# Whole chunks instead of halves in the cached-page attention of a two-layer decoder step

## Chip, cores and metric

The kernel runs on one core of a Trainium2 chip. The metric is the device time of one execution in microseconds (us), here the median over the runs. Below, PE is TensorE's matmuls, PEld its weight loads, DVE is VectorE, ACT is ScalarE, POOL is GpSimd, SP is SyncE, which issues most DMAs.

## The reference, cut to what matters

One inference step of a decoder trunk of two layers, for 256 prompt tokens and 8 samples of 8 new tokens each. A layer is half a SwiGLU network, a mixer, and half a SwiGLU network again. The mixer has three groups of heads (HGRN2, RWKV-7 and MLA attention). The change lies in MLA attention of the samples, which reads a paged cache of 16 pages of 128 tokens for every sample:

```python
def mla_sample_attn(q_nope, q_pe, c, k_pe, ckv_pages, kpe_pages, wuk, wuv):
    c_past = ckv_pages.reshape(B, -1, MLA_KV_RANK)
    kpe_past = kpe_pages.reshape(B, -1, MLA_ROPE)
    q_lat = jnp.einsum('bqhd,rhd->bqhr', q_nope, wuk)
    s_past = jnp.einsum('bqhr,bkr->bhqk', q_lat, c_past) + jnp.einsum('bqhe,bke->bhqk', q_pe, kpe_past)
    ...
    pr = jax.nn.softmax(s, axis=-1)
    o_lat = jnp.einsum('bhqk,bkr->bqhr', pr[..., :P], c_past) + ...
    return jnp.einsum('bqhr,rhd->bqhd', o_lat, wuv)
```

## The kernel before

All matrices are fp32. Activations are kept transposed, 320 tokens wide. A dense product (`dense_steps`, line 398) takes a 128x128 weight block and issues three matmuls of 320 columns on a high and a low part that ScalarE and VectorE split off (`split`, line 422).

**The mixer (line 550) is a weave of streams.** Each stream is a Python generator that emits some instructions and then yields the time at which it may go on, in the kernel's own planning time `self.pe`. `mm` (line 283) adds a planned cost for each matmul: 0.2475 for one of 256 columns onto 64 output rows. `weave` (line 513) takes the first stream of its list whose time has come; where none has, it moves planning time ahead to the earliest. So the order of the instructions in the program is written by due times. A first weave holds `rw` (urgent), `sample`, `fill` (the dense input products of RWKV and HGRN) and `rws`; a second holds `hg` (urgent), `sample`, `prompt` (urgent) and `w_out`. The framework's scheduler then lays that order out for each engine: it takes the program's order as the priority, puts instructions of urgent streams ahead, and takes later instructions where earlier ones are not ready by its own reckoning.

**The sample stream (line 821)** handles the 8 samples in 4 pairs `p`; a pair's cache is 4 chunks `ch` of 4 pages for each of its two samples `si`.

- `scores(p, ch)` (line 851) loads the transposed latents `ct` in tiles of 2 pages of one sample (two DMAs each) and multiplies them with `qlat`: 12 matmuls of 96x256 onto 64 output rows, alternating between the two samples, whose results lie in the two halves of the partitions. Every fp32 matmul is shown as two instructions, so a chunk shows 24.
- `values(p, ch)` (line 892) loads the plain latents `cn`, again in tiles of 2 pages, transposes the exponentials `S` into `PT`, and adds 8 matmuls (16 instructions) onto the accumulator `po` in the bank `pv`.
- `ct` and `cn` have 5 buffers each. A chunk needs 4 tiles of its kind. The order of the stream is four chunks of scores of pair 0, then values of pair p and scores of pair p+1 in turn, then four chunks of values of pair 3 alone. After each pair follow a softmax remainder and the division (lines 944 to 961); at the end the stream loads `wuv` into two `cn` buffers (line 966) and multiplies the result out.

Before the change both kinds go by **halves**: two tiles, then the matmuls that read them. `ready` (line 836) gives a half its due time: 4 pages at 1.05 after the due time of the half before it, or after the planned end of the half three before it, whichever is later; then 2.2 for landing. All page loads are issued by SP. `pages` (line 842) reads the page numbers into SP registers. The last part of the output product that needs the samples (`w_out`, line 590) waits for the end of the stream, the event `smp`.

Of the kernel before, what the change touches and what calls it, by code (L numbers as in the profile page):

```python
# [26 lines left out]
RANK = 256  # L27
# [5 lines left out]
PAGE = 128  # L33
NPAGE = 16
# [2 lines left out]

FBLK, MBLK = 8, 4
LEVELS = [32, 16, 8, 4, 2, 1]
PACE = (0, 1.05)  # L40
ORDER_A = lambda fill, sample: (sample, fill)
ORDER_B = lambda prompt, sample: (sample, prompt)

# [213 lines left out]
class Kern:  # L257
# [563 lines left out]
    def sample(self):  # L821
        nc, l = self.nc, self.l
# [11 lines left out]
        feed = {"ct": [20.0, [], 0], "cn": [20.0, [], 0]}  # L834

        def ready(name, n):
            f = feed[name]
            f[0] = max(f[0], f[1][f[2] - 3] if f[2] > 2 else 0.0) + n * (PACE[1] if f[2] < PACE[0] else 1.05)
            f[2] += 1
            return 0, f[0] + 2.2  # L840

        def pages(i, n):

            with self.tc.issue_after(self.gat[-8].ins) if len(self.gat) >= 8 else ExitStack():
                return nc.values_load_multi_w_load_instructions(
                    self.pti[0:1, i:i + n], engines=[mybir.EngineType.SP], min_val=0, max_val=NPOOL - 1,
                    skip_runtime_bounds_check_because="a page table names pages of the pool")[1]
# [2 lines left out]

        def scores(p, ch):
            ps = self.bank("pa")
            for hf in range(2):
                yield ready("ct", 4)
                self.mark(f"sample{l}")
                cts = []
                for si in range(2):
                    ct = self.s([KR, 2, 3 * PAGE], "ct", 5)
                    i0 = (2 * p + si) * NPAGE + ch * 4 + hf * 2
                    for pg, r in enumerate(pages(i0, 2)):  # L860
                        self.gat.append(nc.sync.dma_start(ct[:, pg, :], ctp[bass.ds(r + l * NPOOL, 1)].rearrange("a p c -> p (a c)")))
                    cts.append(ct)
                for kt in range(3):
                    for si in range(2):
                        self.mm(ps[64 * si:64 * si + 64, hf * 256:hf * 256 + 256], qlat[:KR, kt, 2 * p + si],
                                cts[si][:, :, kt * PAGE:kt * PAGE + PAGE], start=kt == 0, stop=kt == 2)
                feed["ct"][1].append(self.pe)
            S[p, ch] = self.s([128, 512], "S", 5)
            if ch == 0:
                mx[p] = self.s([128, 8], "smx", 2)  # L870
            nc.scalar.copy(S[p, ch], ps)
            nc.vector.tensor_reduce(out=mx[p][:, ch:ch + 1], in_=S[p, ch], axis=AX.X, op=ALU.max)
# [15 lines left out]
        def exps(p, ch):  # L888
            m = mx[p]
            nc.scalar.activation(S[p, ch], S[p, ch], AF.Exp, bias=m[:, 5:6], scale=MLA_SCALE, accum_out=m[:, ch:ch + 1])  # L890

        def values(p, ch, po):
            r0 = ready("cn", 4)
            cns_ = []
            rs = []
            for si in range(2):
                i = (2 * p + si) * NPAGE + ch * 4
                rs.append(pages(i, 4))
            for hf in range(2):
                for si in range(2):  # L900
                    cn = self.s([128, 2, RANK], "cn", 5)
                    for pg in range(2):
                        r = rs[si][hf * 2 + pg]
                        self.gat.append(nc.sync.dma_start(cn[:, pg, :], self.ap["cn"][l, bass.ds(r, 1)].rearrange("a p c -> p (a c)")))
                    cns_.append(cn)
            yield 0, r0[1] - 1.5
            self.mark(f"sample{l}")
            if ch < 3:
                exps(p, ch + 1)
            pt = self.bank("pa")  # L910
            for pg in range(4):
                self.tr(pt[:, pg * 128:pg * 128 + 128], S[p, ch][:, pg * 128:pg * 128 + 128], idt)
            PT = self.s([128, 512], "PT", 2)
            nc.vector.tensor_copy(PT, pt)  # L914
            yield 0, max(self.pe + 1.2, r0[1])
            for hf in range(2):
                self.mark(f"sample{l}")
                for pg in (2 * hf, 2 * hf + 1):
                    for si in range(2):
                        self.mm(po[64 * si:64 * si + 64, :RANK], PT[:, pg * 128 + 64 * si:pg * 128 + 64 * si + 64],  # L920
                                cns_[2 * hf + si][:, pg % 2, :], start=ch == 0 and pg == 0, stop=False)
                feed["cn"][1].append(self.pe)
                if hf == 0:
                    yield ready("cn", 4)

        for ch in range(4):
            yield from scores(0, ch)
# [3 lines left out]
        for p in range(4):  # L931
            po = self.bank("pv")
            exps(p, 0)
            for ch in range(4):
                yield from values(p, ch, po)
                if p < 3:
                    yield from scores(p + 1, ch)
# [31 lines left out]
        for g in range(4):  # L969
            ps = self.bank("pa")  # L970
            for rt in range(2):
                for hh in range(2):
                    h = 2 * g + hh
                    self.mm(ps[64 * hh:64 * hh + 64, :64], wuv[rt][:, h * 64:h * 64 + 64], qlat[:, rt, :, h, :],
                            start=rt == 0, stop=rt == 1)
# [546 lines left out]
```

## Time and profile before

| | us |
|---|---|
| median of 3 runs | 1676.75 (1676.6 to 1680.71) |
| the profiled execution | 1678.2 |
| its span, first to last instruction | 1676.4 |
| PE busy | 1627.8 (97%) |
| PEld busy | 1448.2 (86%) |
| DVE busy | 958.7 (57%) |
| ACT busy | 716.8 (43%) |

The profile is of one execution on the one core. Busy time of PE is the time in which at least one matmul was in flight; matmuls are pipelined, so a busy PE can still be slower than its best. "Idle before" is the time for which an engine had nothing in flight before an instruction, with what released it. In the timeline view one row merges neighbouring instructions of one group: start, length, engine, line, operation, output and inputs, shapes, count. A start-to-start distance between two rows is the time that the first of them really took from the engine.

### The profile page before, as it was taken

The numbers are of one execution on the slowest core, as the hardware profiler recorded it, in microseconds if no ns is written. First come the engines' busy times: TensorE is split into PE (matmuls) and PEld (weight loads), VectorE is DVE, ScalarE is ACT, GpSimd is POOL, SyncE is SP. The second block draws the span as 40 slices with busy tenths as digits, with TensorE's granted clock in tenths as the row PEclk, the third lists the DMA queues.
The fourth block names the chain that finished last, engine by engine and source line by source line (L and its number), as shares of the span: only waits on it lengthen the run. The fifth ranks groups of instructions, "written<-read, shape, count | busy, mean of one in ns | idle before, by whom it ended". The sixth has DMA issues, their size and how long they took to land. (4 is left out here: it accounts for less than half of the span.)

```text
span 1676.4 us, 33385 instructions
## 1 busy us (share of the span) xinstructions
PE 1627.8 (97%) x13174; PEld 1448.2 (86%) x13174; DVE 958.7 (57%) x1599; ACT 716.8 (43%) x1209; POOL 78.3 (5%) x112
## 2 busy tenths in 40 slices
PE   8999999999999899999999999999999998999998
PEld 7999998777557599999999999987765666999998
DVE  7555447844456575554465554478344665655543
ACT  6444334543353354443344443346242543544433
POOL 0000000200031000000000000002000300000000
PEclk9999999999999999999999999999999998999999
DMA  8555526556573454555445555456457545345542
GB/s 268 151 151 149 149 81 175 173 150 178 177 229 112 150 171 149 151 151 151 151 145 149 149 151 150 115 161 185 118 172 217 160 135 180 112 147 147 150 151 93
DMA packets 130908, 260.05 MB, mean 155 GB/s; under 512 B 17264, under 2 KB 75952, under 8 KB 130624
## 3 DMA queue, kind: packets, MB, share of 16 engines
q1 hardware_dynamic: 111584, 223.58, 44.7%
q10 hardware_dynamic: 19136, 34.28, 6.9%
q8 instruction: 104, 1.70, 0.4%
q0 software_dynamic: 32, 0.07, 0.1%
q14 instruction: 52, 0.43, 0.1%
HBM read 253.39 MB, written 4.47 MB: 154 GB/s over the span
## 5 line engine op out<-in xcount | busy, mean ns | idle before, releaser
L423 DVE TENSOR_TENSOR w<-raw,w 128x1024 fp32r<-128x1024 f32 (+1 forms) x392 | 410.0, 1047 | 325.9 <-ACT w L422 319.8
L422 ACT CAST w<-raw 128x1024 fp32r<-128x1024 f32 (+1 forms) x392 | 354.9, 909 | 437.4 <-PE pd L286 190.3
L286 PE MATMUL pd<-xh,w 128*128 128x320 f32 x1792 | 427.6, 317 | 14.4 <-ACT w L422 10.6
L286 PEld LDWEIGHTS pd<-xh,w 128*128 128x128 f32 x1792 | 307.0, 190 | 30.6 <-ACT w L422 14.9
L286 PE MATMUL pd<-xl,w 128*128 128x320 f32 x896 | 282.0, 316 | 0.0
L286 PE MATMUL pr<-xh,w 128*128 128x320 f32 x1056 | 241.7, 311 | 4.4 <-ACT w L422 4.0
L286 PE MATMUL pa<-xh,w 128*128 128x320 f32 x896 | 201.7, 309 | 0.0
L286 PEld LDWEIGHTS pr<-xh,w 128*128 128x128 f32 x1056 | 178.3, 188 | 6.6 <-ACT w L422 5.3
L286 PEld LDWEIGHTS pd<-xl,w 128*128 128x128 f32 x896 | 170.5, 190 | 5.6 <-issue 4.6
L286 PE MATMUL pr<-xl,w 128*128 128x320 f32 x528 | 162.5, 309 | 0.0
L286 PE MATMUL pd<-hh,w 128*128 128x320 f32 x704 | 158.2, 309 | 0.0
L286 PE MATMUL pr<-hh,w 128*128 128x320 f32 x704 | 158.2, 309 | 0.0
L286 PEld LDWEIGHTS pa<-xh,w 128*128 128x128 f32 x896 | 151.0, 188 | 0.0
L286 PE MATMUL pa<-xl,w 128*128 128x320 f32 x448 | 137.6, 309 | 0.0
L286 PE MATMUL pa<-ct,qlat 96*64 96x256 f32 x768 | 119.9, 393 | 0.8 <-ACT w L422 0.4
L286 PEld LDWEIGHTS pd<-hh,w 128*128 128x128 f32 x704 | 118.4, 188 | 0.0
L286 PEld LDWEIGHTS pr<-hh,w 128*128 128x128 f32 x704 | 118.4, 188 | 0.0
L286 PE MATMUL pd<-hl,w 128*128 128x320 f32 x352 | 108.8, 309 | 0.0
L286 PE MATMUL pr<-hl,w 128*128 128x320 f32 x352 | 108.8, 309 | 0.0
L286 PEld LDWEIGHTS pr<-xl,w 128*128 128x128 f32 x528 | 99.1, 188 | 0.4
L470 ACT ACTIVATE fa<-fa 128x320 f32<-128x320 f32 x88 | 41.5, 472 | 134.0 <-DVE fa L469 133.9
L286 PEld LDWEIGHTS pa<-ct,qlat 96*64 96x64 f32 x768 | 59.9, 138 | 38.3 <-issue 14.2
(381 smaller groups left out, 2010.4 us busy)
## 6 DMA issues: line engine op xcount, KB each, us to landing
raw<-in_wf SPq DMA_DIRECT2D x264, 512.0 KB, 3.6
ct<-in_ct SPq DMA_DIRECT2D x256, 144.0 KB, 2.8
raw<-in_wm ACTq DMA_DIRECT2D x128, 256.0 KB, 3.1
cn<-in_cn SPq DMA_DIRECT2D x256, 128.0 KB, 2.4
xT<-in_x SPq DMA_DIRECT2D x4, 320.0 KB, 6.9
wukt<-in_wukt SPq DMA_DIRECT2D x2, 576.0 KB, 6.3
S<-in_rws SPq DMA_DIRECT2D x4, 256.0 KB, 3.5
o_rws<-S SPq DMA_DIRECT2D x4, 256.0 KB, 2.7
```

The source lines that it names most:

```text
L286: self.last = self.nc.tensor.matmul(out, w, x, start=start, stop=stop)
L422: self.cast = nc.scalar.copy(h, src).ins
L423: nc.vector.tensor_tensor(out=lo, in0=src, in1=h.bitcast(F32), op=ALU.subtract)
L470: nc.scalar.activation(a, a, AF.Silu)
```

## The change

`scores` and `values` take a whole chunk at a time: four tiles are loaded, then all matmuls of the chunk follow in one piece, in the reverse order (second half first, second sample first), so that the first matmul reads the tile that was issued last. `ready` gives a chunk its due time as 8 pages at 1.05 after its predecessor's due time or after the planned end of its predecessor's matmuls, whichever is later, plus 2.2. The stream yields once less in each chunk. For the last pair, chunks 1 and 3 of the values take buffers of `ct`. The numbers of loads, matmuls and transposes stay as they are.

```diff
-PACE = (0, 1.05)
+PACE = 1.05
...
         def ready(name, n):
             f = feed[name]
-            f[0] = max(f[0], f[1][f[2] - 3] if f[2] > 2 else 0.0) + n * (PACE[1] if f[2] < PACE[0] else 1.05)
+            f[0] = max(f[0], f[1][f[2] - 1] if f[2] else 0.0) + n * PACE
             f[2] += 1
             return 0, f[0] + 2.2
...
         def scores(p, ch):
             ps = self.bank("pa")
+            yield ready("ct", 8)
+            self.mark(f"sample{l}")
+            cts = []
             for hf in range(2):
-                yield ready("ct", 4)
-                self.mark(f"sample{l}")
-                cts = []
                 for si in range(2):
                     ct = self.s([KR, 2, 3 * PAGE], "ct", 5)
-                    i0 = (2 * p + si) * NPAGE + ch * 4 + hf * 2
-                    for pg, r in enumerate(pages(i0, 2)):
+                    rs = pages((2 * p + si) * NPAGE + ch * 4 + hf * 2, 2)
+                    for pg, r in enumerate(rs):
                         self.gat.append(nc.sync.dma_start(ct[:, pg, :], ctp[bass.ds(r + l * NPOOL, 1)].rearrange("a p c -> p (a c)")))
                     cts.append(ct)
+
+            for hf in (1, 0):
                 for kt in range(3):
-                    for si in range(2):
+                    for si in (1, 0):
                         self.mm(ps[64 * si:64 * si + 64, hf * 256:hf * 256 + 256], qlat[:KR, kt, 2 * p + si],
-                                cts[si][:, :, kt * PAGE:kt * PAGE + PAGE], start=kt == 0, stop=kt == 2)
-                feed["ct"][1].append(self.pe)
+                                cts[2 * hf + si][:, :, kt * PAGE:kt * PAGE + PAGE], start=kt == 0, stop=kt == 2)
+            feed["ct"][1].append(self.pe)
...
         def values(p, ch, po):
-            r0 = ready("cn", 4)
+            r0 = ready("cn", 8)
...
-                    cn = self.s([128, 2, RANK], "cn", 5)
+
+                    cn = self.s([128, 2, RANK], "ct" if p == 3 and ch % 2 else "cn", 5)
...
             yield 0, max(self.pe + 1.2, r0[1])
-            for hf in range(2):
-                self.mark(f"sample{l}")
-                for pg in (2 * hf, 2 * hf + 1):
-                    for si in range(2):
-                        self.mm(po[64 * si:64 * si + 64, :RANK], PT[:, pg * 128 + 64 * si:pg * 128 + 64 * si + 64],
-                                cns_[2 * hf + si][:, pg % 2, :], start=ch == 0 and pg == 0, stop=False)
-                feed["cn"][1].append(self.pe)
-                if hf == 0:
-                    yield ready("cn", 4)
+            self.mark(f"sample{l}")
+            for pg in (3, 2, 1, 0):
+                for si in (1, 0):
+                    self.mm(po[64 * si:64 * si + 64, :RANK], PT[:, pg * 128 + 64 * si:pg * 128 + 64 * si + 64],
+                            cns_[2 * (pg // 2) + si][:, pg % 2, :], start=ch == 0 and pg == 3, stop=False)
+            feed["cn"][1].append(self.pe)
```

## Rows read from the trace of the kernel before

**Rows 1.** Windows by stage: us, busy time of each engine, granted clock, DMA.
```profile
0.00:250.00 250.00, 242.40 (x1631) 241.31 (x1632) 142.00 (x215) 109.84 (x152) 3.10 (x9) 1.00 0.53 159
250.00:592.00 342.00, 327.46 (x3295) 239.06 (x3293) 200.87 (x401) 145.47 (x316) 36.10 (x50) 0.99 0.57 170
592.00:1080.00 488.00, 487.36 (x3315) 486.26 (x3315) 275.81 (x388) 211.25 (x284) 0.00 (x0) 1.00 0.48 144
1080.00:1418.00 338.00, 321.89 (x3248) 233.90 (x3247) 197.73 (x395) 141.15 (x309) 36.12 (x50) 0.97 0.57 167
```

**Rows 2.** What PE waited for: us in total, times, longest.
```profile
PE pa L290 <- ACT S L890: 6.4, 4, 1.9
PE pv L286 <- DMA cn<-in_cn: 4.3, 4, 2.6
PE pa L286 <- DMA ct<-in_ct: 0.4, 1, 0.4
```

**Rows 3.** Timeline of PE, first layer: first sample run, then one whole chunk.
```profile
294.91 1.95 PE L286 MATMUL pa<-ct,qlat 96*64 96x256 f32 x16
...
329.37 0.31 PE L286 MATMUL pd<-xh,w 128*128 128x320 f32 x1
329.61 2.81 PE L286 MATMUL pa<-ct,qlat 96*64 96x256 f32 x24
332.36 0.42 PE L286 MATMUL pd<-xh,w 128*128 128x320 f32 x1
332.61 0.31 PE L286 MATMUL pd<-xl,w 128*128 128x320 f32 x1
332.75 0.45 PE L286 MATMUL pd<-xh,w 128*128 128x320 f32 x2
```

**Rows 4.** Timeline of PE, first layer: one chunk of values, cut up.
```profile
371.08 0.31 PE L286 MATMUL pd<-xh,w 128*128 128x320 f32 x1
371.32 0.65 PE L286 MATMUL pv<-cn,PT 128*64 128x256 f32 x2
371.89 0.68 PE L286 MATMUL pr<-X,rwa 64*64 64x64 f32 x16
372.50 0.65 PE L286 MATMUL pv<-cn,PT 128*64 128x256 f32 x4
373.09 0.68 PE L286 MATMUL pr<-rwa,X 64*64 64x64 f32 x16
```

**Rows 5.** Timeline of PE, first layer: end of the sample stream.
```profile
552.90 1.95 PE L286 MATMUL pv<-cn,PT 128*64 128x256 f32 x16
554.78 0.66 PE L290 MATMUL pa<-cf,S 128*128 128x128 f32 x4
...
567.30 1.32 PE L286 MATMUL pv<-cn,PT 128*64 128x256 f32 x6 [0.62 <-DMA cn<-in_cn]
...
570.57 0.82 PE L286 MATMUL pd<-pPT,V 128*64 128x256 f32 x8
571.95 0.65 PE L286 MATMUL pv<-cn,PT 128*64 128x256 f32 x2 [0.56 <-DMA cn<-in_cn]
```

**Rows 6.** Timeline of PE, second layer: first and last run of sample matmuls.
```profile
1121.09 1.95 PE L286 MATMUL pa<-ct,qlat 96*64 96x256 f32 x16
...
1399.81 0.65 PE L286 MATMUL pv<-cn,PT 128*64 128x256 f32 x2 [2.55 <-DMA cn<-in_cn]
```

**Rows 7.** Timeline of SP, first layer: page loads in mid-stream and at its end.
```profile
452.22 4.90 SPq L904 DMA_DIRECT2D cn<-in_cn  x8
...
540.62 27.13 SPq L904 DMA_DIRECT2D cn<-in_cn  x31
567.85 0.85 SPq L966 DMA_DIRECT2D cn<-in_wuv  x2
568.88 0.34 SPq L904 DMA_DIRECT2D cn<-in_cn  x1
```

**Rows 8.** View of the tile cn: from issue to landing.
```profile
DMA to landing us min/median/max: 1.9/2.4/6.9
```

**Rows 9.** Windows at the ends of both layers' streams: columns as in the first group.
```profile
575.10:578.50 3.40, 3.40 (x22) 2.57 (x16) 0.45 (x2) 0.42 (x2) 0.00 (x0) 0.51 0.00 0
1396.00:1401.00 5.00, 2.45 (x19) 1.11 (x18) 0.85 (x2) 0.37 (x1) 0.00 (x0) 1.00 0.29 93
1401.10:1411.30 10.20, 9.22 (x53) 7.37 (x54) 2.85 (x8) 1.84 (x6) 0.00 (x0) 0.50 0.16 31
```

More of the change, by code (lines that the diff above doesn't have):

```diff
@@ L892, in values @@
         def values(p, ch, po):
-            r0 = ready("cn", 4)
+            r0 = ready("cn", 8)
             cns_ = []
-            rs = []
-            for si in range(2):
-                i = (2 * p + si) * NPAGE + ch * 4
-                rs.append(pages(i, 4))
+            rs = [pages((2 * p + si) * NPAGE + ch * 4, 4) for si in range(2)]
             for hf in range(2):
                 for si in range(2):
-                    cn = self.s([128, 2, RANK], "cn", 5)
+                    cn = self.s([128, 2, RANK], "ct" if p == 3 and ch % 2 else "cn", 5)
                     for pg in range(2):
@@ L915, in values @@
             yield 0, max(self.pe + 1.2, r0[1])
-            for hf in range(2):
-                self.mark(f"sample{l}")
-                for pg in (2 * hf, 2 * hf + 1):
-                    for si in range(2):
-                        self.mm(po[64 * si:64 * si + 64, :RANK], PT[:, pg * 128 + 64 * si:pg * 128 + 64 * si + 64],
-                                cns_[2 * hf + si][:, pg % 2, :], start=ch == 0 and pg == 0, stop=False)
-                feed["cn"][1].append(self.pe)
-                if hf == 0:
-                    yield ready("cn", 4)
+            self.mark(f"sample{l}")
[4 more added lines that the diff above has]
+            feed["cn"][1].append(self.pe)
         for ch in range(4):
```

## The prediction

> **What bounds the kernel now.** I read the windows by stage first, to see where PE loses time at all. The two networks around the mixer leave PE next to nothing to gain: 487.36 of 488.00 us busy. The mixers take 342 and 338 us, with 327.46 and 321.89 busy, so PE stands still for 14.5 and 16.1 us in them [rows 1]. The DMA engines are at 0.57 of their time there, so bandwidth is no bound. PE is the engine to watch, and a change can bring time in two ways: less standing still, or a PE that gets through the same matmuls faster while it counts as busy.
>
> The list of waits comes second. Of the idle time, waits for pages are a small part: 4.3 us for `cn` and 0.4 for `ct` in both layers together; the waits for the exponentials (6.4 us) aren't touched by the change [rows 2]. So what was to be gained from pages that land earlier is under 5 us.
>
> Third, the timeline of PE. A chunk of scores that runs in one piece takes from 329.61 to 332.36, 2.75 us for its 24 instructions or 0.115 each [rows 3]. Such chunks are rare. A chunk of values at 371 us is cut after 2 instructions, then after 4, with matmuls of the RWKV stream between [rows 4]. Taking any unbroken stretch of `ct` or `cn` matmuls as a run, I count 76 runs in the first layer, the first and last being those at 294.91 and 571.95 us [rows 3, 5], and 76 in the second, from 1121.09 to 1399.81 [rows 6]. Whole chunks would need 32 a layer.
>
> Last, the end of the stream, where nothing else is left for PE. In the first layer SP issues the last 32 page loads from 540.62 to 569.22, with only the two `wuv` loads in between [rows 7]; that is 28.6 us or 7.2 for each chunk of 8 loads. In mid-stream 8 loads take SP 4.90 us [rows 7]. So at the end the five `cn` buffers hold the loads back, and PE waits 0.62 and 0.56 us there, in the second layer 2.55 [rows 5, 6].
>
> **The change, part by part.** The sum is made against the profiled execution, 1678.2 us with a span of 1676.4. It lies 1.45 above the median, which I take off at the end. No load, matmul, transpose or copy is added or removed.
>
> *Fewer cuts.* What a cut costs: 2 instructions hold PE from 371.32 to 371.89, 0.57 us where 2 x 0.115 = 0.23 would do, so 0.34 too much; 4 hold it 0.59 where 0.46 would do, 0.13 too much [rows 4]. The mean is 0.24. Going in costs as well: from a dense matmul to a sample matmul it is 0.24 us from start to start, between two dense ones 0.14 to 0.15 [rows 3, 4], so 0.09 more. A cut costs 0.33. Two things cut: a tile that the scheduler doesn't hold for landed when the one before it is (the first matmul then runs alone), and urgent matmuls of other streams. Waiting for the last tile first takes away the first kind only. I take 44 runs a layer, 32 chunks and a dozen urgent cuts: 2 x 32 x 0.33 = 21.1 us less. Bounds: all 44 cuts a layer gone, 29.0; only 12 a layer, 7.9.
>
> *The waits for pages* (4.7 us, [rows 2]) go, since most stood at the stream's end, where the loads will be arranged otherwise; what comes in their place is the next point.
>
> *Later due times.* This works against the change. A half was due 4.2 after the half before, so 8.4 for a chunk. Now a chunk is due 8.4 + 2.2 after the end of the last chunk of its kind and takes 12 x 0.2475 = 2.97 (scores) or 1.98 (values). Sixteen chunks of scores and four of values alone come to at least 16 x 13.57 + 4 x 12.58 = 267 of the planner's own microseconds where 20 x 8.4 = 168 was the pace asked for. The planner fills that time with the other streams, which are then used up earlier, and the sample's chunks slide towards the end. On the chip the stream takes 277 us in the first layer even now (294.91 to 572), so urgent work delays it anyway, and I don't carry over the whole difference. I take it that of the last four chunks of values three have nothing beside them. With two sets of buffers in turn, such a chunk costs SP's 4.90 us for its 8 loads, and PE has 1.88 (552.90 to 554.78) and some 0.66 of transposes to do [rows 5]; 2.4 us stay empty. That is 7.2 a layer, 14.4 in all. Bounds: nothing, if the stream keeps its place, and without turns 4.90 + 2.4 for landing [rows 8] less 2.5 = 4.8 a chunk for all four, 38 us in all.
>
> *The keys' buffers for the last values* let the loads of chunk 1 start as soon as the last scores are done and not after chunk 0 of the values: 4.90 for a chunk in place of 7.2 [rows 7]. This is in the term above already; without it the 2.4 would be 4.6.
>
> *One wait for a chunk.* Scores of a chunk now wait for its 8th load, half of them waited for the 4th: up to half of SP's 4.90 us later. In mid-stream PE has other streams for that time, so I set nothing; without cover it would be 2.45 us a chunk. Queued behind the waiting matmul are the copy of `S` and its maximum, which are needed a whole pair later. On SP the loads of the other kind are queued behind a load that waits for a buffer; three of a chunk's four tiles wait for the chunk before, so both kinds come in bursts of 8. That has the same cover.
>
> *The clock.* Before the second layer's end PE was busy for 2.45 of 5.00 us, and after it the granted clock was 0.50 for 10.2 us, which is 1.2 GHz; in the first layer it was 0.51 for 3.4 us [rows 9]. A thinner end in the first layer may bring one more stretch of 3.4 us at half clock: 1.7 us.
>
> Sum: -21.1 - 4.7 + 14.4 + 1.7 = -9.7. From 1678.2 that is 1668.5, and less 1.45, **1667**.
>
> **The rivals.** *The late stream (slower).* The dense fill is used up early, and the last two pairs of chunks as well as all four chunks of values run bare. A bare pair costs SP 2 x 4.90 = 9.8 us and PE 2.75 + 1.88 + 0.66 = 5.3, so 4.5 idle; with 4 x 2.4 that is 18.6 a layer, 37.2 in all: +37.2 - 21.1 - 4.7 + 1.7 = +13, or 1690. It decides from 12.9 idle us a layer on, where it eats up both gains. For it speaks the sum of due times; against it that the stream is already longer than those due times, and that the scheduler takes ready chunks ahead when PE is free.
>
> *Nothing moves (same).* The cuts are mostly urgent work, as in [rows 4], and stay; 12 fewer a layer give 7.9, and two bare chunks a layer cost 9.6: 9.6 - 7.9 - 4.7 + 1.7 = -1.3, or 1675. For it: both cuts in [rows 4] are followed by RWKV matmuls, which are urgent.
>
> *The low clock (slower).* The bare chunks at the end are short bursts between loads; if PE goes through them and through the part of the output product behind them at 0.50, as after 1401 us, that product (8 tiles of 6 matmuls at 0.15, 7 us) takes twice as long in both layers, while the chunks stay hidden behind their loads: 14 us in place of 1.7, so +2.6 against the profiled time, or 1678 to 1679; with one more bare chunk a layer it is 1684. The Trainium skill ("TensorE: Matmul & The Clock Gate", section on HAM oscillation) says that bursts of matmuls with DMA waits between them start at the low clock every time. The trace agrees for the one stretch it shows, at 1401 us. By that rule the sum would be this rival's and not mine.
>
> **How the numbers follow.** What a measurement of this kernel can tell from no change is 0.3%, 5 us. My forecast gets 0.43; its own range is 1648 to 1672. Nothing moves: 0.18. The late stream: 0.35, the low clock: 0.04; both slower. The two main terms have the same size and opposite signs, so the range has to hold both: from 1647 (all cuts gone, no chunk bare: 1678 - 29 - 4.7 and a little back) to 1700 (the late stream with half of the cuts left). Beyond lies 0.2.
>
> **What the profile after would show.** If the cuts go: chunks of 24 and 16 instructions in one piece, under 50 runs a layer, and fewer busy microseconds of the `ct` and `cn` groups. If the late stream holds: page loads that end later relative to `prompt` and `w_out`, with PE idle and waiting for `cn` in the last 30 us of each mixer. If nothing moves: about 70 runs a layer, with RWKV matmuls between. I am wrong if the mixers shorten by other means than these, or if PE waits for pages in mid-stream, where I set nothing.

## The result and the profile after

The changed kernel takes 1759.57 us (median of 4 runs, 1755.61 to 1766.97) against 1676.67 us in the same comparison: a ratio of 1.0501, interval 1.0481 to 1.0522. It is slower by 83 us. The forecast was 1667, and even the upper end of the range, 1700, lies 60 us below the result. The profiled execution took 1755.61.

The page of the changed kernel, span and engines:

```profile
span 1753.8 us, 33367 instructions
...
PE 1647.9 (94%) x13174; PEld 1476.6 (84%) x13174; DVE 954.0 (54%) x1599; ACT 712.8 (41%) x1203; POOL 78.6 (4%) x112
```

Against before the span grew by 77.4 us. PE stands still for 1753.8 - 1647.9 = 105.9 us where it stood for 48.6, so 57.3 us of the loss is idle time and 20.1 is time in which PE counts as busy. Next, the windows by stage, with the columns of [rows 1]; the mixers now end at about 632 and 1495 us:

```profile
250.00:632.00 382.00, 335.13 (x3267) 250.69 (x3266) 196.27 (x396) 140.96 (x309) 36.16 (x50) 0.91 0.51 150
632.00:1124.00 492.00, 492.00 (x3351) 491.34 (x3350) 279.42 (x394) 213.58 (x287) 0.00 (x0) 1.00 0.49 145
1124.00:1495.00 371.00, 327.17 (x3230) 242.25 (x3229) 193.20 (x393) 138.57 (x305) 36.30 (x50) 0.93 0.51 152
```

The mixers took 342 and 338 us [rows 1]; now they take 382 and 371, and their granted clock fell from 0.99 and 0.97 to 0.91 and 0.93. The network between them is nearly as it was (492 us here, 488 before). What PE waited for (us in total, times, longest), the rows that answer to [rows 2]:

```profile
PE pa L286 <- DMA ct<-in_ct: 42.8, 15, 5.9
PE pv L286 <- DMA cn<-in_cn: 10.7, 6, 4.2
...
PE pv L286 <- DMA ct<-in_cn: 7.8, 2, 3.9
```

Waits for pages were 4.7 us and are 61.3. That is +56.6, about as much as the idle time gained. So the place is found: pages that come too late for PE, in both layers alike (33.2 and 28.1 us). Why they are late is read from two views that group PE's work by what it is. First the stretch from 250 to 400 us, early in the first layer's stream, in the kernel before:

```profile
L286 PE MATMUL pd<-xh,w 128*128 128x320 f32 x185 | 46.6, 324 | 1.4 <-ACT w L422 0.6 <-DVE pe L1002 0.5 <-DVE w L423 0.2
...
L286 PE MATMUL pa<-ct,qlat 96*64 96x256 f32 x168 | 25.6, 390 | 0.0
...
L286 PE MATMUL pv<-cn,PT 128*64 128x256 f32 x48 | 9.1, 395 | 0.0
```

And the same stretch in the changed kernel:

```profile
L286 PE MATMUL pd<-xh,w 128*128 128x320 f32 x260 | 62.1, 318 | 1.1 <-DVE w L423 0.7 <-ACT w L422 0.4
...
L286 PE MATMUL pa<-ct,qlat 96*64 96x256 f32 x120 | 18.4, 393 | 0.0
...
L286 PE MATMUL pv<-cn,PT 128*64 128x256 f32 x16 | 1.9, 379 | 0.0
```

No page is waited for here. PE does other things: 75 more of the dense matmuls `pd<-xh,w`, and of the sample's work two chunks of scores and two of values less (48 and 32 instructions). That work comes back later, when little dense work is left beside it. It begins in mid-stream: from 400 to 470 us, with 24 `pd<-xh,w` where the kernel before has 65, PE waits 11.1 us for pages, in the second layer 10.1 us from 1270 to 1320. Most of it comes at the end, when nothing dense is left. The same grouping from 520 to 620 us, changed kernel:

```profile
L286 PE MATMUL pa<-ct,qlat 96*64 96x256 f32 x144 | 26.6, 525 | 13.8 <-DMA ct<-in_ct 13.8
L286 PE MATMUL pv<-cn,PT 128*64 128x256 f32 x128 | 21.4, 481 | 7.6 <-DMA cn<-in_cn 4.4 <-DVE PT L914 3.1
...
L286 PE MATMUL pv<-ct,PT 128*64 128x256 f32 x32 | 4.5, 426 | 3.9 <-DMA ct<-in_cn 3.9
...
L286 PE MATMUL pd<-xh,w 128*128 128x320 f32 x2 | 0.9, 552 | 0.0
```

Six chunks of scores and ten of values run in these 100 us, and two dense matmuls `pd<-xh,w`. What a pair of chunks costs when it is alone is seen in PE's timeline of that stretch:

```profile
564.42 4.23 PE L286 MATMUL pa<-ct,qlat 96*64 96x256 f32 x24 [3.54 <-DMA ct<-in_ct]
568.58 0.95 PE L290 MATMUL pa<-cf,S 128*128 128x128 f32 x4
570.32 1.95 PE L286 MATMUL pv<-cn,PT 128*64 128x256 f32 x16 [0.78 <-DVE PT L914]
575.76 4.59 PE L286 MATMUL pa<-ct,qlat 96*64 96x256 f32 x24 [3.49 <-DMA ct<-in_ct]
...
588.20 5.32 PE L286 MATMUL pa<-ct,qlat 96*64 96x256 f32 x24 [4.54 <-DMA ct<-in_ct]
```

And in SP's, which issues the loads:

```profile
556.67 5.63 SPq L861 DMA_DIRECT2D ct<-in_ct  x8
562.85 4.54 SPq L904 DMA_DIRECT2D cn<-in_cn  x8
568.09 5.66 SPq L861 DMA_DIRECT2D ct<-in_ct  x8
574.29 5.56 SPq L904 DMA_DIRECT2D cn<-in_cn  x8
580.56 5.63 SPq L861 DMA_DIRECT2D ct<-in_ct  x8
```

A pair takes PE 11.3 and 12.4 us from start to start. SP takes 11.4 and 12.5 us for the 16 loads of a pair, and the rows of loads fill all but some 1.3 us of it. SP hardly waits for buffers here; from 556 to 591 us its list of waits has one row:

```profile
SPq L861 <- PE pv L286: 0.7, 3, 0.3
```

So SP's issue is the bound, and PE waits. The 16 DMA instructions are only part of it, 0.32 to 0.35 us each in most cases, some 5.5 us a pair; reading the page numbers into registers takes 0.47 us six times, 2.8 us. PE is also slow while it works: 24 instructions take 4.23 to 5.32 us where [rows 3] showed 2.81. The windows (columns as in [rows 1]) give the reason:

```profile
520.00:560.00 40.00, 30.26 (x179) 17.58 (x180) 12.58 (x26) 9.78 (x22) 1.32 (x1) 0.70 0.52 150
560.00:600.00 40.00, 25.16 (x155) 18.67 (x151) 6.12 (x15) 5.29 (x14) 0.00 (x0) 0.79 0.65 189
```

The granted clock is 0.70 and 0.79, a mixture of the levels 1.2 and 2.4 GHz, while PE is busy for 30 and 25 us of 40. Within a pair the scores, after a wait of 3.5 us, get the low clock for part of their time, and the values behind them the full one:

```profile
564.40:568.60 4.20, 4.18 (x25) 3.37 (x25) 0.00 (x0) 0.00 (x0) 0.00 (x0) 0.67 0.84 223
570.30:572.30 2.00, 1.95 (x16) 1.05 (x16) 0.56 (x1) 0.00 (x0) 0.00 (x0) 1.00 0.53 155
```

### The profile page after: what moved, and what is told of

It reads as the page before. It is cut to its first block, busy times and chain, and to the rows that moved or that the text cites. A ratio compares the mean times of both kernels' runs of the same rounds, so it can differ in the third digit from the quotient of the medians.

```text
span 1753.8 us, 33367 instructions
## 1 busy us (share of the span) xinstructions
PE 1647.9 (94%) x13174; PEld 1476.6 (84%) x13174; DVE 954.0 (54%) x1599; ACT 712.8 (41%) x1203; POOL 78.6 (4%) x112
## 4 chain that ended last, share of the span: by engine, by line
PE 84%; DMA 5%; SPq 5%; issue 2%; DVE 2%; ACT 2%; DVEq 0%; ACTq 0%
PE pd L286 32%; PE pr L286 29%; PE pa L286 19%; PE pv L286 3%; DMA ct<-in_ct 2%; SPq L861 2%; DMA raw<-in_wm 2%; SPq L845 1%; PE pa L290 1%; SPq L904 1%; PE pd L290 0%; DMA xT<-in_x 0%; DVE w L423 0%; DMA ct<-in_cn 0%; DMA raw<-in_wf 0%
## 5 line engine op out<-in xcount | busy, mean ns | idle before, releaser
L286 PE MATMUL pd<-xh,w 128*128 128x320 f32 x1792 | 420.3, 315 | 13.8 <-ACT w L422 10.0
L286 PE MATMUL pa<-ct,qlat 96*64 96x256 f32 x768 | 129.4, 457 | 42.8 <-DMA ct<-in_ct 42.8
L286 PEld LDWEIGHTS pa<-ct,qlat 96*64 96x64 f32 x768 | 78.8, 161 | 76.0 <-issue 52.1
```

The lines of the kernel that those rows point to most:

```text
L286: self.last = self.nc.tensor.matmul(out, w, x, start=start, stop=stop)
```

## The experiments

Ratios are to the kernel before, run in turn with each on the same chip (medians of 1675.0 to 1677.5 us), with their 95% intervals.

### Undo the due rule in the changed kernel; put the rule alone into the kernel before

**Two back.**

```diff
-            f[0] = max(f[0], f[1][f[2] - 1] if f[2] else 0.0) + n * PACE
+            f[0] = max(f[0], f[1][f[2] - 2] if f[2] > 1 else 0.0) + n * PACE
```

> The changed kernel with one index of the due-time rule put back in spirit: a chunk is due after the planned end of the chunk two before it, not of the one just before (the rule before the change looked three halves back). Whole chunks, the reverse order and the extra buffers stay. Theory A (the due times push the chunks of the sample behind all other work): the last 90 us of a mixer with nothing but sample work on PE shrink to 10 or 20, the time goes back to 1660 to 1695 us. Theory B (whole chunks themselves are the cost: four of five buffers bound to a chunk, so loads and matmuls of a kind can't overlap): the stream stays slow, 1735 to 1760. With A, the time against the kernel before the change also tells what whole chunks are worth by themselves.

Measured: 1690.70 us, 1.0079 [1.0054, 1.0105], in the range of theory A. PE's waits for pages:

```profile
PE pa L286 <- DMA ct<-in_ct: 18.7, 13, 3.1
...
PE pv L286 <- DMA cn<-in_cn: 5.8, 2, 3.3
PE pv L286 <- DMA ct<-in_cn: 5.4, 3, 3.4
```

**Halves, late** (on the kernel before; halves, order and buffers stay):

```diff
-            f[0] = max(f[0], f[1][f[2] - 3] if f[2] > 2 else 0.0) + n * (PACE[1] if f[2] < PACE[0] else 1.05)
+            f[0] = max(f[0], f[1][-1] if f[1] else 0.0) + n * 1.05
...
-                yield ready("ct", 4)
+                yield (0, 0.0) if hf else ready("ct", 8)
...
-            r0 = ready("cn", 4)
+            r0 = ready("cn", 8)
...
-                    yield ready("cn", 4)
+                    yield 0, 0.0
```

> The kernel before the change, still by halves in the old order with the old buffers, but with the new due times: the first half of a chunk is due 8.4 + 2.2 after the planned end of the last half of its kind, the second half at once. Theory A: as slow as the changed kernel, 1740 to 1780 us, with a long stretch of bare sample work at the end of each mixer. Theory B: the time stays within 1% of the kernel before the change, 1665 to 1695, since the halves still overlap.

Measured: 1744.28 us, 1.0397 [1.0369, 1.0426]; 23.8 us of waits for `ct`, 14.1 for `cn`, and 260 dense matmuls `pd<-xh,w` from 250 to 400 us, as many as in the changed kernel. The rule alone costs 69 us on the old kernel, and taking it out of the new one gives back 69. This is the main cause, shown from both sides.

### The order alone undone

```diff
-            for hf in (1, 0):
+            for hf in (0, 1):
...
-                    for si in (1, 0):
+                    for si in (0, 1):
...
-            for pg in (3, 2, 1, 0):
-                for si in (1, 0):
+            for pg in (0, 1, 2, 3):
+                for si in (0, 1):
...
-                            cns_[2 * (pg // 2) + si][:, pg % 2, :], start=ch == 0 and pg == 3, stop=False)
+                            cns_[2 * (pg // 2) + si][:, pg % 2, :], start=ch == 0 and pg == 0, stop=False)
```

> The changed kernel with the matmuls of a chunk in the old order (first half first, first sample first), so that the first matmul waits for the tile that lands first. Theory A: 1755 to 1770 us, no gain from the order, since at the end of the mixer SP's issue of 16 loads a pair sets the pace whichever tile comes first. Theory B: the early matmuls overlap with the later loads again, a pair shortens by up to 2 us, 1730 to 1750. If the reverse order keeps chunks in one piece, as I had forecast, this kernel has more runs than the 55 a layer of the changed one, worth 0.33 us each.

Measured: 1758.34 us, 1.0499 [1.0471, 1.0526]: no difference from the changed kernel, as theory A expected. While the stream is late, the order within a chunk doesn't change the time. PE waits less for pages (39.7 us in place of 61.3) and is busy longer (1671.4 us in place of 1647.9), which fits SP's issue setting the pace either way. The sample matmuls fall into 60 runs in each layer, where the changed kernel shows 55 and 54; by the price of 0.33 these are 4 us, too few to see here.

### The keys' buffers

**Taken out of the changed kernel:**

```diff
-                    cn = self.s([128, 2, RANK], "ct" if p == 3 and ch % 2 else "cn", 5)
+                    cn = self.s([128, 2, RANK], "cn", 5)
```

> The changed kernel without the keys' buffers for the last values: all values take the five cn buffers. Both theories: slower by the loads that can't go ahead in the last four chunks of each mixer, 3 chunks of some 4 us, 10 to 25 us in all: 1770 to 1785. Nothing (1755 to 1765) would say that this part of the change was free.

Measured: 1784.19 us, 1.0638 [1.0615, 1.0662], 25 us above the changed kernel. PE's timeline of the last three chunks of values, first layer:

```profile
599.48 3.26 PE L286 MATMUL pv<-cn,PT 128*64 128x256 f32 x16 [2.65 <-DMA cn<-in_cn]
606.62 3.68 PE L286 MATMUL pv<-cn,PT 128*64 128x256 f32 x16 [3.66 <-DMA cn<-in_cn]
613.58 3.68 PE L286 MATMUL pv<-cn,PT 128*64 128x256 f32 x16 [3.27 <-DMA cn<-in_cn]
```

A chunk takes 7 us here and PE waits before each. I read that as loads and matmuls taking turns on one set of buffers.

**Put alone into the kernel before** (the same line, the other way round):

> The kernel before the change with only the keys' buffers for the last values. Theory A (the keys' buffers pay by letting the last loads run ahead, 25 us in the late stream): the last loads of a mixer end some 5 us earlier; the waits for cn (4.3 us) go, 1666 to 1674 us. Rival (the end of the mixer is set by the prompt's heads as well, so earlier values wait for nothing): 1673 to 1679, no difference.

Measured: 1662.00 us (6 runs, 1661.58 to 1663.67), 0.9925 [0.9903, 0.9946]. This beats both kernels, and is better than either expectation. SP's timeline at the end of the first layer's stream:

```profile
539.34 5.78 SPq L904 DMA_DIRECT2D cn<-in_cn  x8
545.65 4.38 SPq L904 DMA_DIRECT2D ct<-in_cn  x8
550.56 5.03 SPq L904 DMA_DIRECT2D cn<-in_cn  x7
...
557.48 3.99 SPq L904 DMA_DIRECT2D ct<-in_cn  x7
561.57 0.38 SPq L966 DMA_DIRECT2D cn<-in_wuv  x1
562.13 0.72 SPq L904 DMA_DIRECT2D ct<-in_cn  x1
```

The last 32 loads go out from 539.34 to 562.85, 23.5 us, where [rows 7] showed 28.6. PE no longer waits for `cn` at all; 2.1 us of waits for `ct` are left. What went is mainly one stop of SP in each layer. SP's waits for PE's values at the end of the first layer's stream, before (540 to 570 us) and here (539 to 563 us):

```profile
SPq L904 <- PE pv L286: 6.5, 2, 6.3
SPq L904 <- PE pv L286: 1.5, 2, 1.1
```

In the second layer the longest stop goes from 8.1 to 2.6 us.

### The reverse order, in the kernel before

**Inside each half, scores and values:**

```diff
-                    for si in range(2):
+                    for si in (1, 0):
...
-                for pg in (2 * hf, 2 * hf + 1):
-                    for si in range(2):
+                for pg in (2 * hf + 1, 2 * hf):
+                    for si in (1, 0):
...
-                                cns_[2 * hf + si][:, pg % 2, :], start=ch == 0 and pg == 0, stop=False)
+                                cns_[2 * hf + si][:, pg % 2, :], start=ch == 0 and pg == 1, stop=False)
```

> The kernel before the change with only the order reversed inside each half: the half's second tile first. Theory of the cuts (0.33 us each, those by landing go away): about 60 runs a layer in place of 76, 8 to 12 us less, 1664 to 1669. Rival (the cuts don't cost PE time that is short, or they are urgent work): 70 or more runs, or fewer runs at 1673 to 1680.

Measured: 1706.35 us, 1.0193 [1.0167, 1.0219]: 31 us slower, outside both ranges. The runs did become fewer as the theory of the cuts had it, 58 and 66 a layer in place of 76 and 76, but the time went the other way: what the order costs is more than the cuts can give. SP and PE at the end of the first layer's stream, first SP:

```profile
546.94 30.05 SPq L904 DMA_DIRECT2D cn<-in_cn  x31
...
579.80 0.34 SPq L904 DMA_DIRECT2D cn<-in_cn  x1
```

then PE:

```profile
571.80 1.08 PE L286 MATMUL pv<-cn,PT 128*64 128x256 f32 x8 [1.06 <-DMA cn<-in_cn]
573.68 1.88 PE L286 MATMUL pv<-cn,PT 128*64 128x256 f32 x8 [0.80 <-DMA cn<-in_cn]
577.29 1.97 PE L286 MATMUL pv<-cn,PT 128*64 128x256 f32 x8 [1.73 <-DMA cn<-in_cn]
582.24 1.97 PE L286 MATMUL pv<-cn,PT 128*64 128x256 f32 x8 [2.97 <-DMA cn<-in_cn]
```

The last 32 loads take 33.2 us in place of 28.6 [rows 7]; the longest stop among them, in which SP waits for PE's values, is 9.6 us in place of 6.3. And the first of them goes out 6.3 us later than before, so the stream was late ahead of its end already. The two tiles of a half are now read as one block that starts with the second one's landing, and the tile that was loaded first is read last, so that its buffer, the one that the next loads ask for first, comes free late. In the old order PE reads a tile while the next one is landing. That is how I read these rows; no run parts the late start from the late release. PE's waits grow towards the end, and from 573.7 on eight instructions take 1.9 us in place of 1.1: from 572 to 584 us the granted clock was 0.58.

**In the values alone** (the `pg` and last `si` lines of that diff):

> The kernel before with the reverse order inside each half in the values alone; the scores keep the old order. Theory (the reverse order costs where loads wait for buffers, which is the values' end: there a buffer pair comes free late, and of the 23.8 us of waits for cn that the reverse order in both kinds showed, 4.3 were there before): 1692 to 1704, with 18 to 24 us of waits for cn. Rival (the scores' reverse order costs it, or both share it in mid-stream): 1676 to 1686, with under 10 us for cn.

Measured: 1696.12 us, 1.0126 [1.0097, 1.0156], with 19.0 us of waits for `cn` and 8.3 for `ct`. As expected by the theory: some 21 of the 31 us lie in the values, and most of the waits for `cn` come in the last chunks of a layer, after 565 and 1406 us.

### Order and buffers together, and whole chunks in the old order

**Reverse order in the halves with the keys' buffers** (both edits above):

> Both of the last two together, halves and old due times kept: if each gives what its theory says, 1655 to 1665 us, which would beat both kernels; by the rivals 1673 to 1680.

Measured: 1691.61 us, 1.0102 [1.0076, 1.0129], slower than either expectation. The buffers give back 15 of the 31 us, no more.

**Whole chunks, old order, two-back rule, keys' buffers** (the edits of the first and the third experiment in the changed kernel):

> The kernel of e1 (whole chunks, due after the planned end of the chunk two before) with the matmuls in the old order, first tile first. If waiting for the last tile first is what costs the remaining 13 us of e1, since PE stands in a chunk that could begin, this one gets 5 to 15 us faster, 1676 to 1686. If one piece is worth more than an early start, it gets slower, 1693 to 1705, with more runs a layer.

Measured: 1673.55 us (12 runs), 0.9992 [0.9979, 1.0006]: no difference from before. Against the two-back run the old order is worth 17 us, in the direction of the first theory and a little beyond its 5 to 15. Against the halves with the keys' buffers (1662.00) whole chunks and their rule lose 11.5 us. Its sample matmuls fall into 74 and 72 runs in the two layers, hardly fewer than 76 and 76; the two-back run, which differs only in the order, shows 56 and 54. So it is the reverse order that joins the cuts here, and not the chunk. (In the late stream the runs are few in the old order too: 60 and 60 above, and 62 and 64 in halves.)

Put in a row, these runs add up to the change: the kernel before, 1675; with the keys' buffers, 1662; with whole chunks and the two-back rule besides, 1674; with the reverse order, 1691; with the change's own rule, 1760. The steps are -13, +12, +17 and +69 us. No run parts whole chunks from the two-back rule within the 12, and the steps hold in this sequence only: in the late stream the order is worth nothing and the buffers 25.

### What in the rule makes the stream late

**Half the pace**, the changed kernel with

```diff
-PACE = 1.05
+PACE = 0.5
```

> The changed kernel with its rule (8 pages after the end of the chunk before), but 0.5 a page in place of 1.05. A chunk of scores is then planned at 2.2 + 8 x 0.5 + 2.97 = 9.2 in place of 13.6. Theory (the planned period is what makes the stream late): 9.2 is under what SP needs for the 16 loads of a pair, so the stream keeps its place; 1690 to 1710, near the 1690.7 of the two-back rule, with the waits for ct back under 25 us. Rival (it is the chaining to the end of the matmuls, whatever the pace): 1740 to 1760.

Measured: 1748.89 us, 1.0451 [1.0417, 1.0485]. The theory I had then, that the period only has to lie under what SP needs for a pair, fell.

**No pace** (`PACE = 0.0`):

> The changed kernel with its rule (after the end of the chunk before), but nothing a page in place of 1.05: a chunk is due 2.2 after the end of its predecessor, planned at 5.2 for scores in place of 13.6, far under what SP needs. Half the pace (9.2) had still shown 1748.9. Theory (the period is what counts, and 9.2 was still too long, since urgent work between comes on top): the stream keeps its place, the last chunk of scores starts before 560 us in the first layer, and the time is near that of the two-back rule, 1680 to 1700. Rival (it is the tie to the predecessor's end, in which every delay stays, whatever the pace): the last chunk of scores starts after 570 us, 1725 to 1750.

Measured: 1693.94 us, 1.0119 [1.0078, 1.0161]; the last chunk of scores of the first layer starts at 551 us. So the tie to the predecessor by itself isn't it either.

**A quarter of it** (`PACE = 0.25`):

> The changed kernel with its rule and 0.25 a page: a chunk of scores is planned at 2.2 + 8 x 0.25 + 2.97 = 7.2, between the 9.2 that showed 1748.9 and the 5.2 that showed 1693.9, and below the 8.4 of the two-back rule (1690.7). Theory (the tie is harmless once the planned period is under 8.4): 1685 to 1705. Rival (the tie carries every delay along, so that the loss shrinks evenly with the pace, and 7.2 lies half way): 1715 to 1735.

Measured: 1728.55 us, 1.0324 [1.0281, 1.0367]: the rival's value, the loss shrinks step by step with the pace. With a planned 7.2 a chunk, less than the 8.4 of the two-back rule, this kernel is still 38 us slower than that one, so the length of the planned period alone doesn't decide.

**The tie with a running clock:**

```diff
-            f[0] = max(f[0], f[1][f[2] - 1] if f[2] else 0.0) + n * PACE
+            f[0] = max(f[0] + n * PACE, f[1][f[2] - 1] if f[2] else 0.0)
```

> The changed kernel, due at the later of 8.4 after its predecessor's due time and the predecessor's planned end, plus 2.2: the tie to the predecessor stays, but the 8.4 run from due time to due time and not from the end of the matmuls. Theory (what made the stream late is that the 8.4 were added behind the end of the matmuls): near the two-back rule, 1685 to 1705. Rival (the tie itself): over 1715.

Measured: 1700.84 us, 1.0134 [1.0099, 1.0170]: the theory's value. Together:

| due time of a chunk (all with whole chunks, reverse order, keys' buffers) | median, us | dense `pd<-xh,w` from 250 to 400 us |
|---|---|---|
| end of predecessor + 8.4 (the change) | 1759.57 | 260 |
| end of predecessor + 4.0 | 1748.89 | 222 |
| end of predecessor + 2.0 | 1728.55 | 204 |
| end of predecessor + 0 | 1693.94 | 179 |
| due time + 8.4, not before predecessor's end | 1700.84 | 186 |
| later of due time and end of the last but one, + 8.4 | 1690.70 | 192 |

(2.2 for landing come on top in each.) Rows of the last column, each from PE's groups from 250 to 400 us. Half the pace:

```profile
L286 PE MATMUL pd<-xh,w 128*128 128x320 f32 x222 | 54.8, 322 | 0.3 <-DVE w L423 0.3
```

A quarter:

```profile
L286 PE MATMUL pd<-xh,w 128*128 128x320 f32 x204 | 50.8, 323 | 1.2 <-ACT w L422 0.7 <-DVE w L423 0.5
```

No pace:

```profile
L286 PE MATMUL pd<-xh,w 128*128 128x320 f32 x179 | 43.1, 319 | 0.7 <-ACT w L422 0.6 <-DVE w L423 0.2
```

The running clock, then two back:

```profile
L286 PE MATMUL pd<-xh,w 128*128 128x320 f32 x186 | 44.5, 318 | 0.9 <-ACT w L422 0.8 <-DVE w L423 0.2
L286 PE MATMUL pd<-xh,w 128*128 128x320 f32 x192 | 45.8, 318 | 1.0 <-ACT w L422 0.8 <-DVE w L423 0.2
```

What costs is the pace counted behind the end of the matmuls. The same 8.4 counted from due time to due time, under the same tie, cost 59 us less. The kernel before had 185 dense matmuls in this stretch. The rules that stay near that number end between 1690 and 1701 us; those clearly above it spend dense work early that the end then lacks. Between the paces the time doesn't follow the planned period in proportion, and I have no rule for its exact course.

### Earlier due times on the best version

The kernel before with the keys' buffers and

```diff
-PACE = (0, 1.05)
+PACE = (99, 0.8)
```

> The kernel before with the keys' buffers for the last values (1662.0) and 0.8 a page in place of 1.05. Theory (once no chunk runs bare, the pace of the due times is not what is worth time; SP's loads set the stream): 1657 to 1667. Rival (earlier due times shorten the end further): under 1655. Rival (an early sample stream leaves the prompt's work alone at the end): over 1670.

Measured: 1687.08 us, 1.0060 [1.0041, 1.0078], 25 us slower than with 1.05: in the last rival's range, but not by its mechanism. The trace shows waits for pages of 7.0 us, not the 61 of the late stream, and PE busy for 1636.1 us against 1618.4, at a mean granted clock of 0.980 against 0.992. Of the prompt and the sample it is the sample that is left alone at the end. The prompt's last product and the sample's last one on pages, first layer:

```profile
559.89 0.69 PE L286 MATMUL pd<-pPT,V 128*64 128x128 f32 x4
577.12 1.53 PE L286 MATMUL pv<-ct,PT 128*64 128x256 f32 x6 [0.51 <-DMA ct<-in_cn]
```

With 1.05 the sample's last one ended at 565.94 us and the prompt went on until 571.70. With 0.8 the sample goes on for 18 us after the prompt's end, in the second layer as well, the granted clock from 560 to 582 us is 0.73, and from 582 to 592, where the output product begins, 0.54. Why an earlier pace brings the prompt forward and the sample's end back stays open.

More than five buffers of a kind weren't tried; whether they would make the reverse order free stays open. Nor was it tried to issue part of the page loads from a second engine.

## Why the prediction was wrong, point by point

**Later due times: the step that failed.** I had worked out 267 us of planned time where 168 was the pace asked for, and then wrote "I don't carry over the whole difference", because urgent work delays the stream anyway. That is where it went wrong. Urgent delays don't hide the longer period, they add to it: a due time that counts from the end of the matmuls begins anew after each delay, while the old one ran on at its pace and let the stream catch up. The running clock under the same tie (1700.84 in place of 1759.57 us) and the quarter of the pace (slow although its planned period is short) bear this out; the planner's delays themselves stand in no trace. The difference was 99 planned us a layer. Not all of it came through: the rule alone costs 34 us a layer, and the first layer's stream grew from 277 to 321 us. But I had carried over 7.2, with three chunks of values bare; the trace shows six chunks of scores and ten of values from 520 to 620 us with next to nothing dense beside them, and the rule alone measured 69 us against my 14.4, beyond its upper bound of 38.

**The waits for pages** didn't go from 4.7 to nothing, they came to 61.3 us. About half of that is the same error, seen in the list of waits. Without the rule 29.9 us are left (two back), and without the reverse order as well 6.6 (old order, 1673.55 us).

**One wait for a chunk** I set to nothing in mid-stream, with 2.45 us a chunk as the price without cover, and kept that bound out of the range. Where the stream isn't late, the reverse order that makes this wait costs 17 us (whole chunks) and 31 us (halves). I had named the delay of the first matmul and the loads that wait for buffers, and gave both the cover of mid-stream. At the end of the stream that cover is missing even in the kernel before. How the loss divides between the late first matmul and the late buffer isn't shown.

**Fewer cuts** came in part: 55 and 54 runs where I took 44. By my price that is 43 x 0.33 = 14 us in place of 21.1. The price came from one cut chunk and a few distances, and no run tests it by itself. The time doesn't contradict it: in the two-back run, with 56 and 54 runs, PE is busy for 1623.8 us, 4.0 less than before, although its mean granted clock of 0.980 cost (1 - 0.980) x 1689.4 = 34 us of full speed, against (1 - 0.989) x 1676.4 = 18 before. Added up that is up to 19 us of busy time less at equal clock, an estimate, since part of the half-clock time is idle. But the gain is bought with the order, and the order costs more than it brings.

**The keys' buffers** I had counted within the term before, at 2.2 us a chunk. For three chunks in two layers that would be 13 us; alone they measured 13.2 us of gain, and 25 in the late stream. That the numbers agree is luck. I had spread the 28.6 us of [rows 7] evenly over four chunks. In fact SP stands still once in each layer, for 6.3 and 8.1 us, until PE's first values set buffers free; in the first layer it then issues the other 22 page loads and the two `wuv` loads in 15.2 us, about as fast as in mid-stream. The keys' buffers shorten that stop by 5.2 and 5.5 us, which is most of the gain. PE's waits for pages fell by only 2.6 us, and in the second layer the stretch at 0.50 behind the stream's end [rows 9] is gone: from 1384 to 1400 us the granted clock was 1.00. That the buffers would bring this without the rest of the change I didn't say.

**The clock** had 1.7 us. In full-speed terms the changed kernel lost (1 - 0.964) x 1753.8 = 63 us to it, 45 more than before. PE's busy time grew by 20.1 us only. Part of the difference fell into time in which PE stood still, part may be what the joined cuts gave back; no run parts the two.

**The rivals.** The late stream was the right one, with the right place: loads of a pair behind each other on SP, PE waiting in the last part of the mixer. Its sign was not quite met: I had named waits for `cn` in the last 30 us, and the trace shows mostly waits for `ct`, over the last 100. A third of the waits, 21.2 us, even lies in mid-stream, from 400 to 470 and from 1270 to 1320 us, which I had named as a sign of being wrong. Its size was off. I gave it two bare pairs and four values, 18.6 idle us a layer, and in the trace it is 61.3 / 2 = 30.7 us of waits for pages a layer. The low clock I had as a rival of its own with 0.04; it came with the late stream, not in its place. What the Trainium skill ("TensorE: Matmul & The Clock Gate", section on HAM oscillation) says of bursts between DMA waits, that they start at the low clock, the trace bears out for the scores, which begin after waits of 3.5 to 4.5 us and take 4.23 to 5.32 us; the values behind them at 570.32 us take 1.95, as much as [rows 5] show at full clock. The stretch at 1401 us that I had called in agreement is a weaker case: the two matmuls right after the wait of 2.55 us still took 0.65 us at 1.00 [rows 6, 9], and the clock fell only behind them. Had I put the rival's bare stretch at the difference of due times instead of at two pairs, its time would have lain beyond 1700 and the range with it: 99 us are some ten bare pairs of 9.8, 45 idle us a layer at 4.5 each, an estimate.

## What to carry to other kernels

Where a stream of loads is woven into other work, let its due times run on from due time to due time, with the end of the work only as a lower bound, and measure the pace itself, since a faster one cost 25 us here; a pace counted behind the end of the work adds every delay to all that follows, and dense work that could have covered it is spent early. Look for such a loss at the start of a stage, by counting what each engine did there, since the waits show up only later. And before reading the last-landed tile first, see which buffer the next load asks for: here, with five buffers, reading the tile loaded first first was worth 17 and 31 us where the stream wasn't late. An average over a stretch of loads can hide a single stop; look for the stop before pricing each load.

## What was not expected of the hardware

In the bare stretch the one issuing queue is the bound, with 11.4 to 12.5 us for 16 loads, while the DMA engines are at 0.52 to 0.65 of their time. I had priced a bare pair at 9.8 us from the mid-stream row [rows 7]. And in that stretch the granted clock was 0.70 and 0.79 over two windows of 40 us, though PE works for 30 and 25 us of each; a chunk of scores that starts after a wait of 3.5 us or more takes 4.23 to 5.32 us instead of 2.81, while the values behind it run at 1.00.
